# Rotary embedding on one core: rows 1 and 2 loaded by one transfer, and the first store issued without a hold

## The chip, the core and the metric

The kernel runs on one core of a Trainium2 chip. Four parts of the core matter here. VectorE (DVE in the profile) does all the arithmetic. GpSimd (POOL) does no arithmetic in this kernel: its instruction stream issues nearly all transfers between the device memory (HBM) and the on-chip memory (SBUF), and those transfers may change the number type on the way. ScalarE (ACT) and SyncE (SP) issue one transfer each. The transfers themselves are carried by the core's 16 DMA engines.

The metric is the device time of one execution in microseconds (us), lower being better. The kernel before takes 316.18 us, the median of three runs between 316.02 and 316.21.

## The reference

The input `x` has the shape (8, 2048, 16, 64) in float32: 8 batch rows of 2048 positions, 16 heads and 64 numbers per head. `cos` and `sin` have the shape (2048, 32). Neighbouring numbers of a head form a pair, and each pair is turned by the angle of its position:

```
x1 = x_pairs[..., 0]          # even members of the pairs
x2 = x_pairs[..., 1]          # odd members
out1 = x1 * cos - x2 * sin
out2 = x1 * sin + x2 * cos
out = np.stack([out1, out2], axis=-1).reshape(batch, seq_len, num_heads, head_dim)
```

The output has the shape of `x`, in float32. 67.1 MB are read for `x` and 67.1 MB are written.

## The kernel before, in words

A batch row (a "row" from here on) is one element of the first dimension, 2048 x 1024 numbers, 8.4 MB in float32. It is laid out over 128 partitions; a partition holds 16 positions (`K`) of 1024 numbers, 16384 in all. The position of a number inside a partition is `k`. In SBUF a row is kept in bf16, 4096 KB.

The tile `buf` has five slots of a row (`NX`). `at[b]` (line 51) names the slot of row b: row 0 lies in slot 4, rows 1 and 2 in slots 0 and 1, rows 3 and 4 in slots 2 and 3, row 5 again in slot 4, rows 6 and 7 in slots 0 and 1. So row 5 can be loaded only when row 0 has been stored, and rows 6 and 7 only when rows 1 and 2 have been stored.

`load(b, n)` and `store(b, n)` (lines 56 to 60) issue a transfer of n rows from the GpSimd stream, float32 to bf16 and back. `rotate(b)` (line 62) is three VectorE instructions over a row: line 79 writes `qt`, the row times the sine table, line 85 multiplies the row by the cosine table in place, and line 91 adds the swapped `qt` to it. The result stays in the slot, and the store reads it from there.

Each engine works through its own instructions in order. The order is written out by hand (`manual_schedule`, line 93). Waits between engines come from the data: an instruction waits for the transfer that fills its slot, a store for the last write of its row, a load for the store that empties its slot. The GpSimd stream in order is: load 0 (without its first four positions, which ScalarE's queue brings in), `cos`, `sin`, load 1, load 2, store 0, load 3 and 4, load 5, store 1 and 2, store 3, load 6 and 7, store 4 and 5, store 6, store 7 (without its last four positions). A waiting GpSimd instruction holds up all that stand behind it.

The change touches two places. Lines 99 and 100 load rows 1 and 2 as two transfers. And `rotate(1, gate=0)` (line 113) splits row 1's sine product at position 14 (`GATE`) and puts between the two pieces a copy of one number of row 0 onto itself (lines 83 and 84):

```
            if z < nk:
                one = buf[:1, at[gate], 0, :1]
                nc.vector.tensor_copy(out=one, in_=one)
```

That copy is the last write to row 0's slot, so store 0 (line 114) waits for it. A copy of the same kind at line 134 belongs to the end of the kernel and stays.

Of the kernel before, what the change touches and what calls it, by code (L numbers as in the profile page):

```python
# [2 lines left out]

# [4 lines left out]


@with_exitstack  # L10
def kernel(
    ctx: ExitStack,
    tc: tile.TileContext,
    x: bass.AP,
    cos: bass.AP,
    sin: bass.AP,
    out: bass.AP,
):
    nc = tc.nc
    fp32 = mybir.dt.float32  # L20
    bf16 = mybir.dt.bfloat16
    mult = mybir.AluOpType.mult
    add = mybir.AluOpType.add

    B, S, H, D = x.shape
    P = 128
    K = S // P
    D2 = D // 2
    HD = H * D
    NX = 5  # L30
    HEAD = 4
    TAIL = 4
    GATE = 14

    x_t = x.rearrange("b (p k) h d -> p b k (h d)", p=P, k=K)
    out_t = out.rearrange("b (p k) h d -> p b k (h d)", p=P, k=K)
    cos_t = cos.rearrange("(p k) c -> p (k c)", p=P, k=K)
    sin_t = sin.rearrange("(p k) c -> p (k c)", p=P, k=K)

    consts = ctx.enter_context(tc.tile_pool(name="consts", bufs=1))  # L40
    rows_pool = ctx.enter_context(tc.tile_pool(name="rows", bufs=1))
    stage = ctx.enter_context(tc.tile_pool(name="stage", bufs=1))

    cos_sb = consts.tile([P, K * D2], fp32)
    sin_sb = consts.tile([P, K * D2], fp32)
    c_tab = consts.tile([P, K, D], bf16)
    s_tab = consts.tile([P, K, D], bf16)


    buf = rows_pool.tile([P, NX, K, HD], bf16, name="xt")  # L50
    at = [4, 0, 1, 2, 3, 4, 0, 1]

    def place(b, n=1, k0=0, k1=K):
        return buf[:, at[b] : at[b] + n, k0:k1]

    def load(b, n=1, k0=0, k1=K):
        nc.gpsimd.dma_start(out=place(b, n, k0, k1), in_=x_t[:, b : b + n, k0:k1])  # L57

    def store(b, n=1, k0=0, k1=K):
        nc.gpsimd.dma_start(out=out_t[:, b : b + n, k0:k1], in_=place(b, n, k0, k1))  # L60

    def rotate(b, k0=0, k1=K, gate=None, to=None):
        nk = k1 - k0
        xp = buf[:, at[b], k0:k1]
        qt = stage.tile([P, K, HD], bf16, name="qt", tag="work")

        def rows(a):
            return a.rearrange("p k (h e) -> p k h e", h=H, e=D)

        def tab(a, j0=0, j1=nk):  # L70
            return dataclasses.replace(
                a,
                offset=a.offset + (k0 + j0) * D,
                ap=[a.ap[0], [D, j1 - j0], [0, H], [1, D]],
            )


        for a, z in ((0, nk),) if gate is None else ((0, GATE), (GATE, nk)):
            nc.vector.tensor_tensor(  # L79
                out=rows(qt[:, a:z]), in0=rows(xp[:, a:z]), in1=tab(s_tab, a, z), op=mult  # L80
            )
            if z < nk:
                one = buf[:1, at[gate], 0, :1]
                nc.vector.tensor_copy(out=one, in_=one)  # L84
        nc.vector.tensor_tensor(out=rows(xp), in0=rows(xp), in1=tab(c_tab), op=mult)  # L85
        q_swap = dataclasses.replace(
            qt, offset=qt.offset + 1, ap=[qt.ap[0], [2, nk * HD // 2], [-1, 2]]
        )
        x3 = xp.rearrange("p k (a j) -> p (k a) j", j=2)
        y3 = x3 if to is None else to.rearrange("p k (a j) -> p (k a) j", j=2)  # L90
        nc.vector.tensor_tensor(out=y3, in0=x3, in1=q_swap, op=add)  # L91

    with tc.manual_schedule():
        head = stage.tile([P, TAIL, HD], fp32, name="st", tag="work")
        nc.scalar.dma_start(out=head[:, :HEAD], in_=x_t[:, 0, :HEAD])
        load(0, k0=HEAD)
        nc.gpsimd.dma_start(out=cos_sb, in_=cos_t)  # L97
        nc.gpsimd.dma_start(out=sin_sb, in_=sin_t)  # L98
        load(1)
        load(2)  # L100

        nc.vector.tensor_copy(out=buf[:, at[0], :HEAD], in_=head[:, :HEAD])  # L102
        s2 = s_tab.rearrange("p k (i j) -> p (k i) j", j=2)
        nc.vector.tensor_copy(out=s2[:, :, 0], in_=sin_sb)  # L104
        nc.vector.tensor_scalar_mul(s2[:, :, 1], sin_sb, -1.0)  # L105
        nc.vector.tensor_copy(  # L106
            out=c_tab.rearrange("p k (i j) -> p (k i) j", j=2),
            in_=cos_sb.to_broadcast([P, K * D2, 2]),
        )

        rotate(0, 0, HEAD)
        rotate(0, HEAD, K)
        rotate(1, gate=0)
        store(0)
        load(3, 2)
        load(5)
        rotate(2)
        store(1, 2)
        rotate(3)
        store(3)  # L120
        load(6, 2)
        rotate(4)
        rotate(5)
        store(4, 2)
        rotate(6)
        store(6)
        rotate(7, 0, K - TAIL)
        store(7, k1=K - TAIL)

        tail = buf[:, at[3], : 2 * TAIL].rearrange("p k e -> p (k e)").bitcast(fp32)
        tail = tail.rearrange("p (k e) -> p k e", e=HD)
        nc.vector.tensor_copy(out=buf[:1, at[6], 0, :1], in_=buf[:1, at[7], K - 1, :1])  # L134
        rotate(7, K - TAIL, K, to=tail)
        nc.sync.dma_start(out=out_t[:, 7, K - TAIL :], in_=tail)


# [1 line left out]
_INS = ['x', 'cos', 'sin']  # L140
_OUTS = [((8, 2048, 16, 64), 'float32')]


# [23 lines left out]
```

## Time and profile before

| what | value |
|---|---|
| time, median of three runs | 316.18 us |
| time of the profiled execution | 316.17 us |
| its span in the trace | 314.4 us |
| VectorE busy | 215.4 us, 37 instructions |
| GpSimd busy | 8.6 us, 18 instructions |
| HBM read and written | 67.63 MB and 67.11 MB, 429 GB/s over the span |

The span runs from the first to the last recorded event; the time of an execution is 1.77 us longer. The times of single instructions are counted from the start of the span. The transfer rate (GB/s) that the view of the DMA engines prints counts the bytes as they arrive, so that a load, which arrives in bf16, shows half of the rate at which it reads HBM. A GpSimd DMA instruction's own duration is the time that the issue takes, and the time to landing is counted from the start of the issue until all of the transfer has arrived. Line numbers are those of the kernel before.

### The profile page before, as it was taken

To read this page: it belongs to the slowest core of one execution; us is meant where nothing else is said; L and a number is where in the kernel's file an instruction comes from. 1 tells how busy PE (TensorE), PEld (TensorE's weight loads), DVE (VectorE), ACT (ScalarE), POOL (GpSimd) and SP (SyncE) were. 2 spreads that over 40 slices of the span, in tenths; PEclk is the share of its full clock that TensorE was granted. 3 is DMA by queue.
4 is the path that set the end of the run, shared out by engine and by line. 5 is a ranking of instruction groups with operands and counts; after the bars stand their busy time and mean duration, and the time that the engine had idled before them with its cause. 6 is when DMAs were issued, how large, how long until landed. Compare 5 with 4: busy or idle time off the path is not lost.

```text
span 314.4 us, 113 instructions
## 1 busy us (share of the span) xinstructions
DVE 215.4 (69%) x37; POOL 8.6 (3%) x18
## 2 busy tenths in 40 slices
DVE  0029999999999206999999999300009999980550
POOL 3000000100000000000000000000000000000000
DMA  8999999999999999999999999999999999999996
GB/s 253 264 284 200 200 204 263 267 400 417 317 200 200 208 258 200 200 284 517 400 400 475 459 400 400 242 225 200 200 300 434 400 400 534 400 400 400 434 500 267
DMA packets 2688, 102.24 MB, mean 325 GB/s; under 512 B 256, under 2 KB 256, under 8 KB 384
## 3 DMA queue, kind: packets, MB, share of 16 engines
q0 software_dynamic: 2400, 98.04, 96.8%
q10 hardware_dynamic: 144, 2.10, 1.8%
q1 hardware_dynamic: 144, 2.10, 1.6%
HBM read 67.63 MB, written 67.11 MB: 429 GB/s over the span
## 4 chain that ended last, share of the span: by engine, by line
DVE 62%; another core or an unknown queue 17%; DMA 17%; issue 0%; POOL 0%; DVEq 0%; PEldq 0%
DVE xt L91 21%; DVE xt L85 20%; DVE qt L79 20%; DMA out_dram<-xt 10%; DMA sin_sb<-in_sin_dram 7%; POOL xt L57 0%; DVE c_tab L106 0%; POOL cos_sb L97 0%; DVE s_tab L104 0%; DVE s_tab L105 0%; DVE xt L134 0%; DVE xt L84 0%; DVEq L79 0%; PEldq L162 0%
## 5 line engine op out<-in xcount | busy, mean ns | idle before, releaser
L79 DVE TENSOR_TENSOR qt<-xt,s_tab 128x16384 bf16<-128x16384 bf16 (+4 forms) x11 | 69.9, 6360 | 53.7 <-DMA xt<-in_x_dram 53.5
L91 DVE TENSOR_TENSOR xt<-xt,qt 128x16384 bf16<-128x16384 bf16 (+3 forms) x10 | 72.0, 7198 | 0.3
L85 DVE TENSOR_TENSOR xt<-xt,c_tab 128x16384 bf16<-128x16384 bf16 (+2 forms) x10 | 69.9, 6986 | 0.3
L102 DVE CAST xt<-st 128x4096 bf16<-128x4096 f32 x1 | 2.3, 2295 | 15.2 <-DMA st<-in_x_dram 15.2
L60 POOL DMA_DIRECT2D out_dram<-xt x6 | 3.6, 604 | 221.0 <-DVE xt L91 165.3
L134 DVE COPY xt<-xt 1x1 bf16<-1x1 bf16 x1 | 0.1, 144 | 12.0 <-DMA out_dram<-xt 12.0
L57 POOL DMA_DIRECT2D xt<-in_x_dram x6 | 3.8, 635 | 53.1 <-DMA out_dram<-xt 52.3
L104 DVE CAST s_tab<-sin_sb 128x512 bf16<-128x512 f32 x1 | 0.5, 451 | 6.3 <-DMA sin_sb<-in_sin_dram 6.3
L106 DVE CAST c_tab<-cos_sb 128x1024 bf16<-128x1024 f32 x1 | 0.7, 682 | 0.0
L98 POOL DMA_DIRECT2D sin_sb<-in_sin_dram x1 | 0.6, 562 | 0.0
L97 POOL DMA_DIRECT2D cos_sb<-in_cos_dram x1 | 0.6, 554 | 0.0
L105 DVE TENSOR_SCALAR s_tab<-sin_sb 128x512 bf16<-128x512 f32 x1 | 0.4, 441 | 0.0
L84 DVE COPY xt<-xt 1x1 bf16<-1x1 bf16 x1 | 0.1, 136 | 0.0
L151 POOL MEMSET const-float32-0.0<- 128x1 f32 x1 | 0.1, 98 | 0.2 <-issue 0.2
L151 POOL MEMSET const-bfloat16-1.0<- 128x1 bf16 x1 | 0.1, 101 | 0.0
L151 POOL MEMSET const-float32-1.0<- 128x1 f32 x1 | 0.1, 98 | 0.0
L151 POOL MEMSET const-uint8-127<- 128x1 uint8 x1 | 0.1, 98 | 0.0
## 6 DMA issues: line engine op xcount, KB each, us to landing
xt<-in_x_dram POOLq DMA_DIRECT2D x2, 8192.0 KB, 58.7
xt<-in_x_dram POOLq DMA_DIRECT2D x3, 4096.0 KB, 57.4
out_dram<-xt POOLq DMA_DIRECT2D x1, 6144.0 KB, 26.2
xt<-in_x_dram POOLq DMA_DIRECT2D x1, 3072.0 KB, 21.2
st<-in_x_dram ACTq DMA_DIRECT2D x1, 2048.0 KB, 14.5
out_dram<-xt SPq DMA_DIRECT2D x1, 2048.0 KB, 10.2
cos_sb<-in_cos_dram POOLq DMA_DIRECT2D x1, 256.0 KB, 21.3
sin_sb<-in_sin_dram POOLq DMA_DIRECT2D x1, 256.0 KB, 21.4
```

The source lines that it names most:

```text
L57: nc.gpsimd.dma_start(out=place(b, n, k0, k1), in_=x_t[:, b : b + n, k0:k1])
L60: nc.gpsimd.dma_start(out=out_t[:, b : b + n, k0:k1], in_=place(b, n, k0, k1))
L79: nc.vector.tensor_tensor(out=rows(qt[:, a:z]), in0=rows(xp[:, a:z]), in1=tab(s_tab, a, z), op=mult)
L85: nc.vector.tensor_tensor(out=rows(xp), in0=rows(xp), in1=tab(c_tab), op=mult)
L91: nc.vector.tensor_tensor(out=y3, in0=x3, in1=q_swap, op=add)
L97: nc.gpsimd.dma_start(out=cos_sb, in_=cos_t)
L98: nc.gpsimd.dma_start(out=sin_sb, in_=sin_t)
L102: nc.vector.tensor_copy(out=buf[:, at[0], :HEAD], in_=head[:, :HEAD])
L104: nc.vector.tensor_copy(out=s2[:, :, 0], in_=sin_sb)
L105: nc.vector.tensor_scalar_mul(s2[:, :, 1], sin_sb, -1.0)
L106: nc.vector.tensor_copy(out=c_tab.rearrange("p k (i j) -> p (k i) j", j=2), in_=cos_sb.to_broadcast([P, K * D2, 2]),)
L151: nc = _bacc.Bacc("TRN2", target_bir_lowering=False, num_devices=1)
```

## The change

Rows 1 and 2, which are neighbours in HBM and in `buf`, are loaded by one transfer of 8192 KB in place of two of 4096 KB. Whoever waits for row 1 now waits for the end of that one transfer. `rotate` loses the gate: the sine product of row 1 is one instruction again, and the copy of line 84 is gone. `store(0)` stands before `rotate(1)` in the program, and its only wait on VectorE is for the last addition of row 0.

```
-    def rotate(b, k0=0, k1=K, gate=None, to=None):
+    def rotate(b, k0=0, k1=K, to=None):
...
-        for a, z in ((0, nk),) if gate is None else ((0, GATE), (GATE, nk)):
-            nc.vector.tensor_tensor(
-                out=rows(qt[:, a:z]), in0=rows(xp[:, a:z]), in1=tab(s_tab, a, z), op=mult
-            )
-            if z < nk:
-                one = buf[:1, at[gate], 0, :1]
-                nc.vector.tensor_copy(out=one, in_=one)
+        nc.vector.tensor_tensor(out=rows(qt[:, :nk]), in0=rows(xp), in1=tab(s_tab), op=mult)
...
-        load(1)
-        load(2)
+        load(1, 2)
...
         rotate(0, 0, HEAD)
         rotate(0, HEAD, K)
-        rotate(1, gate=0)
         store(0)
+        rotate(1)
         load(3, 2)
         load(5)
         rotate(2)
```

The helper `tab`, which names a stretch of a table, is shortened to match.

More of the change, by code (lines that the diff above doesn't have):

```diff
@@ L32 @@
     TAIL = 4
-    GATE = 14
     x_t = x.rearrange("b (p k) h d -> p b k (h d)", p=P, k=K)
@@ L68, in rows, with tab @@
             return a.rearrange("p k (h e) -> p k h e", h=H, e=D)
-        def tab(a, j0=0, j1=nk):
+        def tab(a):
             return dataclasses.replace(
-                a,
-                offset=a.offset + (k0 + j0) * D,
-                ap=[a.ap[0], [D, j1 - j0], [0, H], [1, D]],
-            )
-        for a, z in ((0, nk),) if gate is None else ((0, GATE), (GATE, nk)):
-            nc.vector.tensor_tensor(
-                out=rows(qt[:, a:z]), in0=rows(xp[:, a:z]), in1=tab(s_tab, a, z), op=mult
-            )
-            if z < nk:
-                one = buf[:1, at[gate], 0, :1]
-                nc.vector.tensor_copy(out=one, in_=one)
+                a, offset=a.offset + k0 * D, ap=[a.ap[0], [D, nk], [0, H], [1, D]]
+            )
+        nc.vector.tensor_tensor(out=rows(qt[:, :nk]), in0=rows(xp), in1=tab(s_tab), op=mult)
         nc.vector.tensor_tensor(out=rows(xp), in0=rows(xp), in1=tab(c_tab), op=mult)
```

## The prediction

> **What bounds the kernel now.** I read the page first, its busy shares and its DMA queues, and then the waits.
>
> ```profile
> span 314.4 us, 113 instructions
> DVE 215.4 (69%) x37; POOL 8.6 (3%) x18
> DMA  8999999999999999999999999999999999999996
> q0 software_dynamic: 2400, 98.04, 96.8%
> ...
> DVE qt L79 <- DMA xt<-in_x_dram: 53.5, 2, 37.4
> DVE xt L134 <- DMA out_dram<-xt: 12.0, 1, 12.0
> ```
>
> VectorE is busy for 69% of the span only, and it waits for loads (53.5 us in two waits) and for a store (12.0 us). The DMA engines are busy in every slice, and one queue, the one that GpSimd fills, holds 96.8% of the span. So the transfers are the bound. The chain of waits puts 62% on VectorE, but VectorE's long chains end in waits for transfers, and so those chains have room. The question is whether the transfers ever stop, and whether the change makes or removes such a stop.
>
> For that I took the instructions around the change in order of time, and the DMA issues one at a time with their time to landing.
>
> ```profile
> 45.28 6.56 DVE L91 TENSOR_TENSOR xt<-xt,qt 128x12288 bf16<-128x12288 bf16 x1
> 51.88 7.63 DVE L79 TENSOR_TENSOR qt<-xt,s_tab 128x14336 bf16<-128x14336 bf16 x1
> 59.42 0.14 DVE L84 COPY xt<-xt 1x1 bf16<-1x1 bf16 x1
> 59.48 1.20 DVE L79 TENSOR_TENSOR qt<-xt,s_tab 128x2048 bf16<-128x2048 bf16 x1
> 59.85 0.54 POOL L60 DMA_DIRECT2D out_dram<-xt  x1 [55.77 <-DVE xt L84]
> 60.38 0.72 POOL L57 DMA_DIRECT2D xt<-in_x_dram  x1
> 82.22 0.56 POOL L57 DMA_DIRECT2D xt<-in_x_dram  x1 [21.11 <-DMA out_dram<-xt]
> 104.62 0.71 POOL L60 DMA_DIRECT2D out_dram<-xt  x1 [21.84 <-DVE xt L91]
> 120.40 8.69 DVE L79 TENSOR_TENSOR qt<-xt,s_tab 128x16384 bf16<-128x16384 bf16 x1 [16.08 <-DMA xt<-in_x_dram]
> ...
> xt<-in_x_dram POOLq DMA_DIRECT2D x1, 4096.0 KB, 40.0
> xt<-in_x_dram POOLq DMA_DIRECT2D x2, 4096.0 KB, 49.5
> out_dram<-xt POOLq DMA_DIRECT2D x1, 22.1
> xt<-in_x_dram POOLq DMA_DIRECT2D x1, 8192.0 KB, 59.9
> xt<-in_x_dram POOLq DMA_DIRECT2D x1, 4096.0 KB, 57.4
> out_dram<-xt POOLq DMA_DIRECT2D x1, 73.7
> ```
>
> The last six lines are, in order: load 1 alone, loads 1 and 2 together, store 0, load 3 and 4, load 5, store 1 and 2. Issue plus time to landing gives each landing. Load 1: 2.97 + 40.0 = 43.0. Load 2, issued at about 3.5: 49.5 is the mean of 40.0 and its own 59.0, so it lands at 62.5. Store 0: 59.85 + 22.1 = 82.0. Load 3 and 4: 60.38 + 59.9 = 120.3. Load 5: 82.22 + 57.4 = 139.6. Store 1 and 2: 104.62 + 73.7 = 178.3. The later issues (50.8 us for store 3, issued at 146.84; 57.6 for load 6 and 7, issued at 178.60; 75.7 for store 4 and 5, issued at 199.20; 31.5 for store 6, issued at 262.72) land at 197.6, 236.2, 274.9 and 294.2.
>
> From one landing to the next that is 19.5 (load 2), 19.5 (store 0), 38.3, 19.3, 38.7, 19.3, 38.6, 38.7 and 19.3. In the order of issue, each row takes 19.3 to 19.5 us and a pair of rows twice that, whenever it was issued. This says two things: the queue is served first come, first served, and it never runs dry between 43 and 294 us. A third view says the same in 40 slices of the stretch from 24 to 308 us:
>
> ```profile
> DMA  9999889999999999999999899999999999999998
> GB/s 222 222 222 222 194 342 425 443 222 222 222 222 222 222 222 222 443 443 443 443 443 388 369 425 295 222 222 222 222 295 443 443 443 443 443 443 443 406 402 378
> ```
>
> 222 in bf16 is 444 read from HBM, and stores write at 443: there is one ceiling for both directions. The end hangs on this queue. Line 134 starts at 294.20, when store 6 has landed, and the last transfer lands at 303.35 + 10.2 = 313.6.
>
> **The change part by part.** I count against the profiled execution, 316.17 us (span 314.4 and 1.77 around it), which stands 0.01 below the median of the three runs.
>
> *Gate and copy removed.* VectorE loses 0.14 us for the copy, and the split product (51.88 to 60.72 with the copy, 8.84) becomes one of 8.69 with its 0.03 of issue: 0.12 us saved, all of it ahead of VectorE's 16.08 us of idle time at 120.40, so 0 at the end.
>
> *Row 1 waits for row 2's transfer.* The wait is new. Row 1 could start at 51.88, with its data there since 43.0; now it needs the merged load, which ends where load 2 ended, at 62.5 by the ceiling. VectorE starts 0.07 to 0.12 us after a landing (236.2 to 236.27, 120.28 to 120.40), so at 62.6, 10.7 us later. Nothing else is queued on VectorE but rows 1 and 2. Three instructions at 8.72 take 26.2 a row: row 1 ends at 88.8 and row 2 at 114.9 in place of 104.3. The idle time before row 3 covers that, and 5.5 us are left. If that cover were gone, row 3 to row 5 would slip too; they end at 198.9 and meet the next idle time, 37.37 us before row 6 at 236.27. Cost 0.
>
> Who waits for rows 1 and 2? Store 1 and 2, on GpSimd, is issued 0.3 after row 2, at 115.2 in place of 104.62. The queue reaches it when load 5 has landed, at 139.6: 24.4 us to spare. Behind it on GpSimd stands store 3, which waits for row 3 until 146.84 anyway, and is reached at 178.3. Cost 0.
>
> *Store 0 and load 3 and 4 issued earlier.* Row 0 ends at 51.84, so GpSimd issues store 0 at about 52.1 and load 3 and 4 at 52.7. The stream then waits with load 5 for store 0's landing, as before. Both issues lie ahead of landing 62.5, and the queue is served in order, so neither moves a byte ahead. What they can remove is a gap between load 2 and store 0. Store 0's interval is 19.45 before rounding, against 19.3 for the stores and loads that were queued long before their turn. Ends: 0 and -0.15; I take -0.1, since the issue at 59.85 stands only 2.6 us before its turn, the shortest lead of any. Below, in the other direction, an early store may disturb the end of the load beside which it waits; the slowest row interval (19.5) against the quickest (19.3) bounds that at +0.2. The nearest row is load 3 and 4, behind which load 5 and store 1 and 2 lay queued at once, and it took 38.3: I take 0.
>
> *One transfer fewer.* GpSimd's issue takes 0.72 in place of 1.11, with 48 us of waiting behind it: 0. For the queue, a single row takes one fixed cost F and the work w, a pair 2w and one F, so F is twice a single less a pair. With means of 19.4 and 38.6 that is 0.2; with the extremes, from 2 x 19.3 - 38.7 = -0.1 to 2 x 19.5 - 38.3 = 0.7. I take -0.1, between none and the means, because all landings are rounded and the F of these means is no larger than their scatter.
>
> Sum: 0 + 0 - 0.1 - 0.1 = -0.2, so 316.0 us. With all gains at their ends (-0.15 - 0.7) it is 315.3; with the losses (+0.2 and +0.1) 316.5.
>
> **Where a rule and the rows differ.** The rows put F at 0.2 us. The Trainium skill, on the page "DMA: Bandwidth & Descriptors", section "Anatomy of one DMA — SWDGE (gpsimd) path", gives every transfer issued from GpSimd a fixed cost of about 2.0 us beside its bytes. If that cost lay in the queue, one transfer fewer would be worth 2.0, and the sum would be 314.1. The rows of this case speak against it: the landings of adjacent transfers leave no room for 2 us, and so such a cost must pass beside the data of the next transfer.
>
> **The rivals.**
>
> *The join of the two loads is dear (faster).* The two loads meet at 43.0, just behind the tables and the head, and only a mean of two times fixes load 2's landing, so the profile bounds the join less well there than later. Worth the 0.7 of the extremes it gives 315.5, and together with the 0.15 of the store 315.3. The interval of 19.5 that holds the join is at most 0.2 above the others, so I give little to it. With the fixed cost that the Trainium skill states on that page, this rival would give 314.2.
>
> *VectorE's late row becomes the bound (slower).* The place is the wait of line 79 on the merged load. If the 10.7 us passed through to the end, the time would be 316.17 + 10.7 - 0.1 = 326.8. It decides from the point where rows 1 and 2 end after 137, because store 1 and 2 must be in the queue by 139.6 less the lead of 2.6; each further us is then a us of empty queue. The merged load would have to land 22 us late for that. Against it: 114.9 is well short of 137, and the pair of rows 3 and 4, the same form of transfer, took twice a single row.
>
> *The early store slows the loads (slower, slightly).* From 52 us on, two more transfers lie in the ring. If that made every one of the 13 row intervals from 43 to 294 us as slow as the slowest (19.5 against 19.35), it would cost 13 x 0.15 = 2 us: 318.1. Against it, the ring held load 3 and 4, load 5 and store 1 and 2 at 105 us, and the pace was the usual one.
>
> *The store does not come early after all.* If store 0 still waited for something near 60 us, only -0.1 would be left: 316.1, no change.
>
> **How the numbers follow.** About 0.2% (0.63 us) is what a measurement of this kernel can tell from no change, so "same" is 315.5 to 316.8. The forecast, a full queue in the same order, gets 0.75; the store that does not come early 0.04, also same. A dear join gets 0.08, faster. VectorE as the bound gets 0.04, and a ring that slows 0.09, of which most would be slower by under 1 us. That is faster 0.08, same 0.79, slower 0.13. The forecast alone spans 315.3 to 316.5 by its bounds. For 8 in 10 I reach to the milder slow cases: 315.3 to 317.0.
>
> **What would show it.** Right: store 0 issued at about 52.1 and load 3 and 4 at 52.7; an idle time of about 10.7 us on VectorE before row 1, ended by the load; row 1's first product at 62.6; store 1 and 2 at about 115.2; row 3 still at 120.3 to 120.4; row 6 still at 236.1 to 236.3; line 134 at 294.0 to 294.2. Wrong: a merged load that lands away from 62.5, a row 3 or row 6 that starts earlier or later than that by over 0.6 us, a slice of the DMA view that falls below 8 between 24 and 300 us, or row intervals away from 19.3. The prediction falls if the rate of a full queue depends on what is in it, since that is the one thing that the trace of before shows for its own order only.

## The result, and the profile after

The changed kernel takes 317.35 us, the median of six runs between 317.27 and 317.46, against 316.12 for six runs of the kernel before. The ratio is 1.0039, with a 95% interval from 1.0027 to 1.0052. It is slower by 1.2 us, and the prediction (316.0, at most 317.0) missed it.

The page of the changed kernel's profile, its span, busy shares and main queue:

```profile
span 315.7 us, 109 instructions
DVE 215.3 (68%) x35; POOL 8.3 (3%) x17
DMA  8999999999999999999999999999999999999996
q0 software_dynamic: 2384, 98.04, 96.8%
```

The span is 1.3 us longer (315.7 against 314.4), with the same bytes and the same picture of a queue that never rests. On a page with slices of 7.9 us a loss of 1.2 us can't be seen. The instructions in order of time show where it lies:

```profile
45.22 6.56 DVE L81 TENSOR_TENSOR xt<-xt,qt 128x12288 bf16<-128x12288 bf16 x1
52.08 0.57 POOL L59 DMA_DIRECT2D out_dram<-xt  x1 [48.35 <-DVE xt L81]
52.64 0.71 POOL L56 DMA_DIRECT2D xt<-in_x_dram  x1
63.78 8.69 DVE L74 TENSOR_TENSOR qt<-xt,s_tab 128x16384 bf16<-128x16384 bf16 x1 [12.00 <-DMA xt<-in_x_dram]
83.32 0.56 POOL L56 DMA_DIRECT2D xt<-in_x_dram  x1 [29.96 <-DMA out_dram<-xt]
116.40 0.71 POOL L59 DMA_DIRECT2D out_dram<-xt  x1 [32.52 <-DVE xt L81]
121.68 8.69 DVE L74 TENSOR_TENSOR qt<-xt,s_tab 128x16384 bf16<-128x16384 bf16 x1 [5.58 <-DMA xt<-in_x_dram]
```

Store 0 and load 3 and 4 are issued at 52.08 and 52.64, just as the change says. But row 1 starts at 63.78, where 62.6 was forecast, and from row 3 on every row starts 1.3 us later than before: row 3 at 121.68 (120.40 before), row 6 at 237.56 (236.27), line 123, which was line 134, at 295.50 (294.20). So the whole loss arises before 63.8, and nothing after it adds to it or gives any of it back.

The DMA issues, one at a time, with their time to landing: the merged load, store 0, load 5, and store 1 and 2.

```profile
xt<-in_x_dram POOLq DMA_DIRECT2D x1, 8192.0 KB, 60.7
out_dram<-xt POOLq DMA_DIRECT2D x1, 31.0
xt<-in_x_dram POOLq DMA_DIRECT2D x1, 4096.0 KB, 57.6
out_dram<-xt POOLq DMA_DIRECT2D x1, 63.2
```

The merged load, issued at 2.98, lands at 63.7 in place of 62.5. Store 0 lands at 52.08 + 31.0 = 83.1, which is 19.4 later, the usual interval. Load 5 lands at 140.9, and store 1 and 2 at 179.6, 38.7 later. So only the end of the merged load is late.

The packets show which part of it. A transfer of a row reaches the 16 DMA engines as rounds of 16 packets, one for each engine, and the fine view from 56 to 68 us (slices of 0.3 us) marks a round where it begins. First the kernel before, then the changed one:

```profile
DMA  0099000000990000000990000009900000099000
GB/s 0 0 328 1420 0 0 0 0 0 0 328 1420 0 0 0 0 0 0 0 2622 874 0 0 0 0 0 0 2840 655 0 0 0 0 0 0 2621 874 0 0 0
```

```profile
DMA  0099000000990000000000995000009950000099
GB/s 0 0 546 1201 0 0 0 0 0 0 437 1311 0 0 0 0 0 0 0 0 0 0 1529 1748 218 0 0 0 0 0 1529 1748 218 0 0 0 0 0 1529 1748
```

The marks at 56.6 and 59.0 are the last two rounds of the load, about 1750 GB/s when their two slices are summed; the ones that follow, of twice the size, are store 0. Before, the store's first round begins eight to nine slices after the last round of the load. After the change it is eleven to twelve. In the records of the single packets, the 16 packets of that last round take 2.43 us each in the kernel before and 3.17 to 3.86 in the changed one, 3.55 in the mean. The packets of all other rounds of rows 1 to 6 keep their 2.43 to 2.47.

So one round of packets is slower on every DMA engine: the last one of the load that stands ahead of the first store. The queue is never empty there, and that is why the shares show nothing.

### The profile page after: what moved, and what is told of

Read it like the earlier page. It is cut to its first block, busy times and chain, and to the rows that moved or that the text cites. A ratio compares the mean times of both kernels' runs of the same rounds, so it can differ in the third digit from the quotient of the medians.

```text
span 315.7 us, 109 instructions
## 1 busy us (share of the span) xinstructions
DVE 215.3 (68%) x35; POOL 8.3 (3%) x17
## 4 chain that ended last, share of the span: by engine, by line
DVE 61%; another core or an unknown queue 17%; DMA 17%; issue 0%; POOL 0%; DVEq 0%; PEldq 0%
DVE xt L81 21%; DVE xt L75 20%; DVE qt L74 20%; DMA out_dram<-xt 10%; DMA sin_sb<-in_sin_dram 7%; POOL xt L56 0%; DVE c_tab L95 0%; POOL cos_sb L87 0%; DVE s_tab L93 0%; DVE s_tab L94 0%; DVE xt L123 0%; DVEq L74 0%; PEldq L151 0%
## 5 line engine op out<-in xcount | busy, mean ns | idle before, releaser
L74 DVE TENSOR_TENSOR qt<-xt,s_tab 128x16384 bf16<-128x16384 bf16 (+2 forms) x10 | 69.8, 6982 | 55.1 <-DMA xt<-in_x_dram 55.0
```

What stands on the lines that cost most here:

```text
L74: nc.vector.tensor_tensor(out=rows(qt[:, :nk]), in0=rows(xp), in1=tab(s_tab), op=mult)
```

## The experiments

For the tests I had two first theories. A: the store that lies queued behind the running load costs the time. B: the merged load costs it. A measure that leaves out where a run begins is the time from the start of the tables' first instruction on VectorE to the start of row 3. It is 120.40 - 23.85 = 96.6 us before and 121.68 - 23.78 = 97.9 after. A time that stands without a ratio and an interval is that of a single execution; for those runs the argument rests on the packets and on this measure, and not on the time alone.

### Each part of the change alone

**The merged load with a held store.** The hold is an unused product ahead of row 1, in time that VectorE has free.

```
-        load(1)
-        load(2)
+        load(1, 2)
...
-        rotate(1, gate=0)
+        hold = stage.tile([P, K, HD], bf16, name="qt", tag="work")
+        nc.vector.tensor_tensor(
+            out=hold[:, :GATE], in0=buf[:, at[0], :GATE], in1=buf[:, at[0], :GATE], op=mult
+        )
+        one = buf[:1, at[0], 0, :1]
+        nc.vector.tensor_copy(out=one, in_=one)
         store(0)
+        rotate(1)
```

> Loads 1 and 2 merged, but store 0 still held: a product of 14336 numbers that nobody uses and the copy onto row 0 stand ahead of row 1, so that store 0 and load 3 and 4 are issued at about 59.9 as before. Theory A (the store that lies early behind the running load costs the 1.2 us): the merged load lands at 62.4 to 62.5, row 3 starts at 120.4, time 316.1. Theory B (the merged load costs it): it lands at 63.7, row 3 starts at 121.7, time 317.3.

Measured: 316.15 us against 316.06, a ratio of 1.0001 (0.9992 to 1.0010). Its instructions in order of time:

```profile
59.89 0.58 POOL L60 DMA_DIRECT2D out_dram<-xt  x1 [56.16 <-DVE xt L117]
62.35 8.69 DVE L79 TENSOR_TENSOR qt<-xt,s_tab 128x16384 bf16<-128x16384 bf16 x1 [2.75 <-DMA xt<-in_x_dram]
120.31 8.69 DVE L79 TENSOR_TENSOR qt<-xt,s_tab 128x16384 bf16<-128x16384 bf16 x1 [5.64 <-DMA xt<-in_x_dram]
```

Row 1 starts at 62.35 and row 3 at 120.31. The merged load costs nothing, and the late row 1 costs nothing. It gains nothing that can be measured either. Theory B falls. By the fixed 2.0 us a transfer of the Trainium skill ("DMA: Bandwidth & Descriptors", "Anatomy of one DMA — SWDGE (gpsimd) path") one transfer fewer would have been worth 2.0 us if that cost lay in the queue. Where the transfers follow each other in a full queue, this measurement shows none of it.

**The early store with two loads.** The changed kernel, with rows 1 and 2 loaded by two transfers as before.

```
-        load(1, 2)
+        load(1)
+        load(2)
```

> Loads 1 and 2 stay two transfers, the gate and its copy are gone, store 0 is issued at 52.1. Theory A (early store): load 2's last packets are stretched, row 3 starts at 121.7, time 317.3. Theory B (merged load): row 3 at 120.4, time 316.1.

Measured: 317.31 us against 316.06, ratio 1.0035 (1.0023 to 1.0048); row 3 starts at 121.41. The packets of load 2's last round take 3.15 to 3.78 us. So the loss comes with the early issue and needs no merged load. Row 1 runs from 51.90 here, so an idle VectorE has no part in it.

**Store 0 early, load 3 and 4 held.** Both were issued early by the change, so the second could be the cause.

```
         store(0)
+        hold = stage.tile([P, K, HD], bf16, name="qt", tag="work")
+        nc.vector.tensor_tensor(
+            out=hold[:, :14], in0=buf[:, at[0], :14], in1=buf[:, at[0], :14], op=mult
+        )
+        nc.vector.tensor_copy(out=buf[:1, at[3], 0, :1], in_=hold[:1, 0, :1])
         rotate(1)
         load(3, 2)
```

> As the changed kernel, with store 0 at 52.1, but load 3 and 4 is held until about 59.6 by an unused product and a write of one number into row 3's slot. If the store alone costs the time: row 1 starts at 63.8, row 3 at 121.7, time 317.3. If it is load 3 and 4, queued behind the store while the first loads still run: row 1 at 62.5, row 3 at 120.4, time 316.1.

Measured: 317.37 us, row 1 at 63.74, row 3 at 121.64, with load 3 and 4 issued at 60.10. The store alone does it.

### How early is too early

Three kernels like the one before, with the hold at another position.

```
-    GATE = 14
+    GATE = 8      # and 12, and 13
```

> The kernel before with the hold at position 8 in place of 14, so store 0 is issued at about 56.6, some two and a half rounds of packets before its turn at 62. Theory A with a cost that needs only that the store is queued before the last round: row 3 at 121.7, time 317.3. Theory A with a cost that grows with the lead: between 316.1 and 317.3. Theory B: 316.1, row 3 at 120.4.

> The kernel before with the hold at 12 in place of 14: store 0 is issued at about 58.8, so its descriptors come at about 60, when the last round of load 2 (59.3 to 62) is already under way. If the cost needs the store to be queued before the last round begins: 316.1, row 3 at 120.4. If any lead of over 2 us will do: 317.3, row 3 at 121.6.

> The kernel before with the hold at 13: store 0 issued at about 59.4, between 58.87 (last round of load 2 stretched by 0.6 us in the mean) and 59.85 (not stretched). If the cost is the overlap of the store with that round: stretched by about 0.3, row 3 at 120.7, time 316.4 to 316.6. If it is a yes or no of whether the store is queued before some point: 316.1 or 317.3.

Measured, with the packets of the last round ahead of store 0 from the packet records:

| hold at | store 0 issued at | packets of the last round, us | time, us | tables to row 3, us |
|---|---|---|---|---|
| 14 (before) | 59.85 | 2.43 | 316.12 | 96.6 |
| 13 | 59.32 | 2.43 to 2.69, mean 2.49 | 316.23 | 96.6 |
| 12 | 58.87 | 2.71 to 3.32, mean 3.06 | 317.49 | 97.8 |
| 8 | 56.70 | 3.21 to 3.91, mean 3.47 | 317.29 | 97.6 |
| none (after) | 52.08 | 3.17 to 3.86, mean 3.55 | 317.35 | 97.9 |

Over the 16 engines the last round begins at 59.1 to 59.7 us, and in the run at 12 at 59.7 to 60.2. So a store that is issued as the round begins (13) stretches it by 0.06 us in the mean, and one that is issued 0.8 to 1.3 us ahead of it (12) by 0.6. Further ahead adds less and less: 1.04 when it is issued about one round ahead (8) and 1.12 when it is three rounds ahead (after). Of what I had expected at 13, a cost of 0.3 us did not come; a yes or no is nearer, almost none at 13 and more than half at 12. It is a steep edge with a narrow slope, and its points at 13, 12 and 8 are one execution each. The run at 12 has a loss of its own besides: about 0.4 us of it lies in rounds between 37 and 55 us, before the store was issued, and its cause is open. With that taken off it fits between its neighbours.

### Why only this switch

The later switches from loads to stores have their stores queued just as early. Store 1 and 2 was issued at 104.62 in the kernel before, 35 us ahead of its turn behind load 5, and no round there is longer than 2.43 us. Either store 0 is special because it is the first, or something else is at 62 us.

**A small store first.** 64 zeros a partition to a place that the last store overwrites, once from GpSimd and once, in float32, from SyncE.

```
+        wee = consts.tile([P, D], bf16, name="wee")
+        nc.vector.memset(wee, 0.0)
+        nc.gpsimd.dma_start(out=out_t[:, 7, K - 1, :D], in_=wee)
         load(0, k0=HEAD)
```

> The changed kernel with one small store more: 64 numbers a partition of zeros (bf16 to float32) to a place of the output that the last store overwrites, issued by GpSimd ahead of its first load. So store 0 is no longer the first store of the program. If the 1.2 us belong to the first store alone: row 1 starts at 62.5, row 3 at 120.4, time 316.1 to 316.6 with the small store's own cost. If they belong to any store queued early at that point: 63.8, 121.7, and 317.3 to 317.8.

> The same, with the small store in float32 and issued by SyncE, so on another queue. If the cost is that of the core's first write to the output, on whatever queue: row 1 at 62.5, time 316.1 to 316.6. If it is that of the first store on GpSimd's queue: row 1 at 63.8, time 317.3 to 317.8.

Measured: 317.29 against 316.12, ratio 1.0036 (1.0022 to 1.0050), row 1 at 64.08 and row 3 at 122.08; and 317.30 with row 1 at 63.61. A first small store helps on neither queue, so it is not the first write to the output as such.

**Store 0's turn moved to 100 us.** Load 3 and 4 is issued at the start, behind load 1 and 2.

```
         load(1, 2)
+        load(3, 2)
...
         rotate(1)
-        load(3, 2)
         load(5)
```

> The changed kernel with load 3 and 4 issued right behind load 1 and 2, so that store 0, issued at 52, has its turn at about 100 and not at 62. If the first store is stretched wherever its turn is: row 1 starts at 62.5, load 3 and 4 lands some 1.2 us late, at 102.1 in place of 100.9, and the last packets before the store are stretched. If it is the time or the place near 62: no round of packets at 100 is stretched. The order of the later transfers changes with it, so the total says little.

Measured: 321.65 us. Row 1 starts at 62.52, so the switch from one load to another at 62 is free. The rounds from 95 to 107 us, in the fine view, hold the switch from load 3 and 4 to store 0; those from 136 to 148 the switch from load 5 to store 1 and 2:

```profile
DMA  0990000009900000000099500000995000009950
...
DMA  9000005990000089900000000099950000999500
```

In both there is a gap of eleven to twelve slices between the last round of the load and the first of the store, where rounds of a load lie eight slices apart. The packets ahead of store 0 take 2.88 to 3.70 us. So the stretch follows the first store to 100 us and has nothing to do with the time or with row 2. The second stretch (3.11 to 3.92 us) was not expected. It stands at a switch that is free in both kernels, and one thing is different there: GpSimd was held by load 5's wait for store 0 until 121.70, so that the queue had run empty. The first round of load 5 begins 5.0 us after the last of store 0, where 2.45 is usual. That first round is slow as well: its packets take 2.62 to 3.39 us. On the engine that ends last, 2.5 us of empty queue, 0.4 of this slow round and the two stretches (1.1 and 1.5) make up the 5.5 us of this run's loss.

**The first store in pieces.** The thought was that each DMA engine reads the first packet of the store ahead while the last packet of the load still runs; then a small first packet would cost little.

```
-        store(0)
+        store(0, k1=1)     # and k1=8, k0=8
+        store(0, k0=1)
```

> The changed kernel with store 0 in two transfers, the first of one position of 16, the second of the other 15, both issued at 52. Theory C (the DMA engines read the first packet of the queued store ahead, while the last packet of the load still runs, and the cost is the size of that packet): a sixteenth of 1.2, so row 1 at 62.6, row 3 at 120.5, time 316.2 to 316.4. Theory D (the switch from loads to an early store costs 1.2 us whatever its packets are): 63.7, 121.7, 317.3.

> The same, with pieces of 8 and 8 positions. Theory C: half of 1.2, row 1 at 63.1, row 3 at 121.0, time 316.7. Theory D: 63.7, 121.7, 317.3.

Measured: 317.43 against 316.17, ratio 1.0042 (1.0026 to 1.0059), row 1 at 63.76; and 317.39 with row 1 at 63.70. In the first, the small piece was issued at 32.36, as soon as its position was rotated, and not at 52 as I wrote. The packets ahead of the store take 3.07 to 3.72 and 3.20 to 3.94 us. The size of the store's first packet does not matter, and theory C falls.

**A larger store ahead of all loads.** Zeros of four positions, 2048 KB, from a slot that is not yet in use.

```
+        wee = buf[:, at[3], :TAIL]
+        nc.vector.memset(wee, 0.0)
+        nc.gpsimd.dma_start(out=out_t[:, 7, K - TAIL :], in_=wee)
         load(0, k0=HEAD)
```

> The changed kernel with a store of 2048 KB more, zeros for four positions of row 7 that the last store overwrites, ahead of the first load. It costs its own 4.8 us, so every later time moves by about 4.8. If the cost belongs to the first switch from loads to stores since the queue began, and a store of full size ahead of the loads does away with it: row 1 at 67.3, no packet of the merged load stretched, time 320.9. If the switch at row 0 costs the same regardless: row 1 at 68.5, the last packets of the merged load take 3.2 to 3.9 us, time 322.1.

Measured: 322.56 us. The tables' first instruction comes at 30.23, row 1 starts at 68.86 and row 3 at 126.81: 96.6 us from the tables to row 3, as in the kernel before. The time fits neither of the two that I had given, since I had left out the later start. No packet of the merged load takes over 2.44 us, although store 0 was issued at 58.52, 6.4 us before the last round ahead of it began:

```profile
30.23 0.45 DVE L96 CAST s_tab<-sin_sb 128x512 bf16<-128x512 f32 x1 [13.88 <-DMA sin_sb<-in_sin_dram]
68.86 8.69 DVE L74 TENSOR_TENSOR qt<-xt,s_tab 128x16384 bf16<-128x16384 bf16 x1 [10.64 <-DMA xt<-in_x_dram]
126.81 8.69 DVE L74 TENSOR_TENSOR qt<-xt,s_tab 128x16384 bf16<-128x16384 bf16 x1 [5.62 <-DMA xt<-in_x_dram]
```

The store moves everything by 6.4 us, its own 4.8 and a later start for the zeros, and does away with the 1.2. Three more runs tell what about it does that: the large store followed by an empty queue, a load of the same size in its place, and a smaller store.

```
+        wee = buf[:, at[0], HEAD : HEAD + TAIL]            # load 0 must wait for this store
+        nc.vector.memset(wee, 0.0)
+        nc.gpsimd.dma_start(out=out_t[:, 7, K - TAIL :], in_=wee)
...
+        wee = buf[:, at[3], :TAIL]
+        nc.vector.memset(wee, 0.0)
+        nc.gpsimd.dma_start(out=wee, in_=x_t[:, 7, K - TAIL :])   # a load in place of the store
...
+        wee = buf[:, at[3], :1]
+        nc.vector.memset(wee, 0.0)
+        nc.gpsimd.dma_start(out=out_t[:, 7, K - 1 :], in_=wee)    # one position
```

> As the run with the large store first, but the zeros lie where load 0 is to land, so that load 0 and all behind it on GpSimd wait until the large store has landed: the queue runs dry between the two. From the start of the tables' first instruction to the start of row 3 it is 96.6 us without the cost and 97.9 with it. If the cost comes at the first switch from loads to stores since the queue last ran dry: 97.9. If one large store at any earlier time does away with it: 96.6.

> The control: a load of the same 2048 KB of float32, into a slot not yet in use, in place of the large store, with the same set-up and the same later start. If a store is what does away with the cost: from the tables to row 3 97.9 us, and the last packets of the merged load stretched. If the later start or the changed beginning does it: 96.6.

> The store ahead of the loads with one position of 16 (512 KB in place of 2048 KB; 64 numbers did not help). 96.6 us from the tables to row 3 if that is enough to do away with the cost, 97.9 if not.

Measured (328.32, 322.23 and 317.60 us), by the starts of the tables and of row 3, here from the instructions of the run with the empty queue:

```profile
34.72 0.45 DVE L96 CAST s_tab<-sin_sb 128x512 bf16<-128x512 f32 x1 [18.24 <-DMA sin_sb<-in_sin_dram]
74.62 8.69 DVE L74 TENSOR_TENSOR qt<-xt,s_tab 128x16384 bf16<-128x16384 bf16 x1 [11.90 <-DMA xt<-in_x_dram]
132.56 8.69 DVE L74 TENSOR_TENSOR qt<-xt,s_tab 128x16384 bf16<-128x16384 bf16 x1 [5.61 <-DMA xt<-in_x_dram]
```

the run with the load in place of the store:

```profile
28.66 0.47 DVE L96 CAST s_tab<-sin_sb 128x512 bf16<-128x512 f32 x1 [17.81 <-DMA sin_sb<-in_sin_dram]
126.51 8.69 DVE L74 TENSOR_TENSOR qt<-xt,s_tab 128x16384 bf16<-128x16384 bf16 x1 [5.64 <-DMA xt<-in_x_dram]
```

and the run with one position:

```profile
25.32 0.46 DVE L96 CAST s_tab<-sin_sb 128x512 bf16<-128x512 f32 x1 [13.48 <-DMA sin_sb<-in_sin_dram]
121.84 8.69 DVE L74 TENSOR_TENSOR qt<-xt,s_tab 128x16384 bf16<-128x16384 bf16 x1 [5.60 <-DMA xt<-in_x_dram]
```

That is 97.8, 97.9 and 96.5 us. With an empty queue behind the large store the stretch is back, with packets of 3.42 to 3.95 us, and the first round of load 0, right behind the empty queue, is slow too (2.04 to 2.76 us, where its other rounds take 1.83). With a load in the store's place it is there, with 3.39 to 3.78. With a store of 512 KB it is gone. So what does away with it is a store of some size, earlier in the same unbroken run of the queue; 512 KB are enough and 64 numbers a partition (32 KB on arrival) are not. The number of packets does not decide it, for both of these stores have 128, of 4096 and of 256 bytes; whether their bytes or their packets' size does, no run tells. None of these kernels is a way out: the smallest store that helps puts the tables 1.5 us later, and the time is 317.60.

**What follows.** In these runs the cost comes once in each unbroken run of the queue, at the first switch from loads to a store that was issued 0.8 us or more before the last round of the load began. It is 1.0 to 1.5 us. A store that is issued during that last round, as the hold of the kernel before has it, does not pay. Later switches don't pay either. What inside the DMA engines does this stays open: that the switch needs a store already queued, and that it is paid once, is shown; that some state of the engines that an empty queue resets lies behind it would fit, and is not shown. The slow first rounds of a load behind an empty queue (2.62 to 3.39 us in the run with store 0's turn at 100 us, 2.04 to 2.76 in the one with the large store) may belong to the same state; no run tests it.

## Why the prediction was wrong, step by step

- *What bounds the kernel.* Right. The queue is served in order, it is never empty between 43 and 294 us in either kernel, and a delay in it goes to the end one for one: 1.2 us at 63.7 and 1.3 at 295.5.
- *Gate and copy removed.* Right at 0, and of no weight in the runs.
- *Row 1 waits for row 2's transfer.* Right as a mechanism: the idle time before row 1 is 12.00 us (10.7 forecast, and the 1.2 of the late load), store 1 and 2 is issued at 116.40 (115.2 and 1.2), row 3 still waits for its load. The held merged load shows the price: 1.0001.
- *One transfer fewer, -0.1.* Nothing of it can be seen: 316.15 against 316.06 in the run that has only that, with an interval (0.9992 to 1.0010) too wide for 0.1 us. The rival of a dear join falls with it.
- *Store 0 issued earlier, -0.1.* This is the step that failed. I looked for a gap between load 2 and store 0 that an earlier issue could close; there is none that matters: by the packets the store begins 0.03 us in the mean after the load's last round. The disturbance of the running load by the early store was named and bounded at +0.2, by the scatter of the row intervals, and taken as 0 because load 5 and store 1 and 2 lay queued behind load 3 and 4 at no cost. It measured +1.2, all of it in the last round of the load ahead (3.55 us in the mean in place of 2.43). The row that I took as the nearest was the wrong kind: every early queued store in the trace of before comes after a store has already passed, and store 0, the only one that comes first, was the only one queued late. The trace of before held no row for a first store that is queued early, so the scatter of other rows was no bound.
- *The rival of an early store that slows the loads* was right in its cause and wrong in its form. I spread it over 13 row intervals, 318.1 us, and gave it 0.09. It is a single round of packets, and all later intervals are unchanged (19.3 to 19.4 a row).
- *The prediction falls if the rate of a full queue depends on what is in it.* That sentence came near to what happened; no chance stood beside it, the nearest rival had 0.09, and the range ended 0.35 us below the measured time.

Most of the signs of being wrong that the prediction named did come. The merged load lands at 63.7 in place of 62.5, and row 3 starts 1.3 us late, where 0.6 was allowed. In the view of the changed kernel from 24 to 308 us the slice from 59.5 to 66.6 us falls below 8:

```profile
DMA  9999979999999999999999999999999999999999
```

It is a coarse mark, for the view counts all of a packet's time in the slice in which the packet begins, and the same slice held an 8 before.

One reading in the prediction was off and had no weight. The 443 and 444 GB/s count three whole rounds in a slice of 7.1 us; a row of 8.39 MB in 19.3 us is 435 GB/s, in both directions.

## What to carry to other kernels

When a copy or a wait seems to do nothing but hold a transfer back, look for what the transfer would stand beside if it came earlier, and whether the trace has a case of just that kind: same direction, same place in the queue's history. A queue that is full all the time can still lose time in one round of packets, and it is the spacing of the rounds that shows it; the busy share of the page did not. In a kernel that is bound by one queue of loads and stores, issue the first store while the last packets of the load ahead of it are already running, or test both orders.

## What was not expected of the hardware

A packet moves 64 KB on the side of the HBM. It takes 2.43 us on each DMA engine in rows 1 to 6 of both kernels, load or store, one transfer or two, to within 0.04 us; but the last round of loads ahead of the first store takes 3.2 to 3.9 us if the store was already queued. The edge lies between an issue 0.8 to 1.3 us ahead of that round (58.87 us) and one as it begins (59.32). An empty queue brings the cost back, and a store of 512 KB ahead of the loads takes it away.
